# Spreading three reciprocal roots along the tokens by transfers through a line in DRAM instead of float32 products

## The chip, the cores and the metric

The kernel runs on one core of one Trainium2 chip. The metric is device time in microseconds (us) of one execution. The core has a matrix engine (TensorE: PE for the products, PEld for its weight loads), VectorE (DVE), ScalarE (ACT), GpSimd (POOL) and SyncE (SP). SP, ACT and POOL each issue DMA transfers in the order of their own instructions.

## The reference

One layer of a bidirectional encoder, for 512 tokens of width 2048. The input is normed, projected once, and split into queries, keys, values, a gate for attention, the input of a linear recurrence (LRU) and its gate. Attention and the recurrence (forwards and backwards) run side by side; each result is normed over its 1024 channels, gated and projected back.

```python
def rms_norm(x, w):
    xf = x.astype(jnp.float32)
    y = xf * lax.rsqrt(jnp.mean(xf * xf, axis=-1, keepdims=True) + EPS)
    return (y * w.astype(jnp.float32)).astype(x.dtype)

h = rms_norm(x, norm_w)
proj = jnp.einsum('bsd,de->bse', h, w_in)
q, k, v, g_attn, xr, g_lru = jnp.split(proj, SPLITS, axis=-1)
attn_out = attention_group(q, k, v, q_norm_w, k_norm_w)
lru_out = lru_group(xr, conv_w, conv_b, lru_wa, lru_ba, lru_wx, lru_bx, lru_lambda)
mixed = jnp.concatenate([rms_norm(attn_out, attn_norm_w) * jax.nn.silu(g_attn),
                         rms_norm(lru_out, lru_norm_w) * jax.nn.silu(g_lru)], axis=-1)
return x + jnp.einsum('bse,ed->bsd', mixed, w_out)
```

Three of these norms concern us: that of the input `x`, that of `lru_out` and that of `attn_out`. Each needs one reciprocal root per token.

## The kernel before

**Products.** Every float32 product is made of three products of float32r operands (`mm3`, lines 145 to 147): each operand is split into a rounded part (cast on ACT, line 204) and the rest (subtraction on DVE, line 205). Weights come in blocks of 256 rows by 512 columns (`wload`, a 512 KB transfer on SP's queue, line 193, three buffers `wr`). A projection (`proj_feat`, `proj_tok`) accumulates over eight such blocks in the four PSUM banks `pj`; the other four banks are `mm`.

**Order of the program.** The start loads `x` in eight chunks (line 223; the first in two halves), turns them on PE (`xturn`, line 230) and multiplies meanwhile (`a1`: LRU input, first half; the first products are line 287). 13 and 6 products on constants (`busy`, line 923) lie ahead of them, and the 16 rows of `norm_w` (`nw_st`, issued by ACT at line 937) are turned into the columns `nw`, which scale `x`. Then come the recurrences (`lru_half`, twice, woven into the next projections), keys and values (`kv`, woven into the query projections), attention (woven into the gate projections), and the output projection with fewer products than the plain one (`outputs`, line 890, with sums of weight blocks `ts` made by POOL's transfers in DRAM, lines 735 and 738).

**Norms.** A root is first a tile of 128 partitions by 4: token `t*128 + p` is at partition `p`, column `t`. The products need it along the free dimension and on all partitions. `rows` does this: four DVE instructions multiply the identity by a column each (line 265), one float32 product with ones spreads the diagonal over all partitions (line 267), and DVE copies it from PSUM (line 268). It runs three times: for `rbc` (root of the input, used by `evac_bc`, line 366), and twice for `gbc` (root of the LRU group, used by `normed`, line 655, on the tiles `hs`; later root of the attention group, on `av`). The roots themselves are made on POOL (lines 256 and 257). For the two groups, the sums over channels are products with a column of ones (`group_rstd`, line 643), four for every tile of squares; `lru_squares` leaves two such tiles, the halves of `hsum`.

**What sets the order.** PE's order is that of the text. SP's, ACT's and DVE's orders are that of the text in the first part of the start (scopes `s1`, `s2`) and in the output projection; elsewhere a scheduler orders by priority (`high_priority` moves a step ahead of its place) among what can be issued. Buffers of a tag are handed out in the order of the text. The tag `k2` of the pool `lru` has 12 buffers; its first tile is the diagonal of `xstats`, and the next are the gate weights `gr` of `lru_half` (lines 376 and 377, two 128 KB transfers for each of four blocks), which have a priority 600 steps ahead of their place. Each DMA from SP and ACT takes the next of eight semaphores (`DMAHW0` to `DMAHW7`) and waits until the transfer that had it before has landed.

Of the kernel before, what the change touches and what calls it, by code (L numbers as in the profile page):

```python
# [10 lines left out]
F32 = mybir.dt.float32  # L11
F32R = mybir.dt.float32r
AF = mybir.ActivationFunctionType
ALU = mybir.AluOpType
AX = mybir.AxisListType

P = 128
SEQ = 512
DM = 2048
KT = DM // P  # L20
NT = SEQ // P
# [34 lines left out]
def hybrid_kernel(  # L56
# [20 lines left out]
    nc = tc.nc  # L77
# [4 lines left out]
    pools, order = {}, {"left": [], "right": []}  # L82

    def opened(name, side):
        pools[name] = tc.alloc_tile_pool(name=name, bufs=1, side=side, reuse_waits="tile")
        order[side].append(name)
        return pools[name]
# [16 lines left out]
    dp = ctx.enter_context(tc.tile_pool(name="dp", bufs=1, space=bass.MemoryType.DRAM))  # L104
# [3 lines left out]
    def nm(s):  # L108
        cnt[0] += 1
        return f"{s}_{cnt[0]}"  # L110
# [4 lines left out]
    def work():  # L115
        return ("lru", LRU_K2, LRU_B4) if "lru" in pools else ("att", ATT_K2, ATT_B4)

    def k2(dt=F32, shape=(P, SEQ)):
        pool, n, _ = work()
        return pools[pool].tile(list(shape), dt, tag="k2", bufs=n, name=nm("k2"))  # L120
# [14 lines left out]
    def mm():  # L135
        return ps.tile([P, SEQ], F32, tag="mm", name=nm("mm"))

    def const(shape, name, dt=F32):
        return cp.tile(list(shape), dt, tag=name, name=name)

    def f(ap):
        return ap.bitcast(F32)
# [7 lines left out]
    ident = const([P, P], "ident")  # L150
    make_identity(nc, ident)
    ones = const([P, P], "ones")
# [101 lines left out]
    def rsqrt_mean(dst, src, n, width):  # L254

        nc.gpsimd.tensor_scalar(dst, src, 1.0 / n, EPS, op0=ALU.mult, op1=ALU.add)
        nc.gpsimd.tensor_tensor(dst, dst, nhalf[:, :width], op=ALU.pow)

    rstd = const([P, NT], "rstd")
    rbc = const([P, SEQ], "rbc")  # L260

    def rows(dst, col, dg):

        for t in range(NT):
            nc.vector.tensor_scalar(dg[:, t, :], ident, col[:, t : t + 1], None, op0=ALU.mult)
        pb = mm()
        nc.tensor.matmul(pb, ones, dg.rearrange("p t q -> p (t q)"), start=True, stop=True)
        nc.vector.tensor_copy(dst, pb)

    def xstats():  # L270
        s = const([P, NT], "xsum")
        nc.vector.reduce_sum(s, ssq, axis=AX.X)
        rsqrt_mean(rstd, s, DM, NT)
        rows(rbc, rstd, k2(shape=(P, NT, P)))

# [80 lines left out]
    sums = {}  # L358
# [93 lines left out]
    def lru_squares():  # L452

        hsum = pools["rot"].tile([P, 2, SEQ], F32, tag="hsum", name="hsum")
        nc.scalar.activation(hsum, hp[0], AF.Square)
        for pair in hp[1:]:
            yield 2
            sq = pools["rot"].tile([P, 2, SEQ], F32, tag="hsq", bufs=1, name=nm("hsq"))
            nc.scalar.activation(sq, pair, AF.Square)
            nc.vector.tensor_add(hsum, hsum, sq)  # L460
        sums["l"] = [hsum[:, k, :] for k in range(2)]


    def rope_consts():
# [25 lines left out]
    def norm_rope(es, nh, tab):  # L490

        es = [e[:, : nh * HD].rearrange("p (h d) -> p h d", d=HD) for e in es]
        rs = []
        for e in es:
            r = pools["rot"].tile([P, nh], F32, tag=f"rr{nh}", bufs=NT, name=nm("rr"))
            for h in range(nh):
                sq = pools["rot"].tile([P, HD], F32, tag="sh", bufs=1, name=nm("sh"))
                nc.scalar.activation(sq, e[:, h, :], AF.Square, accum_out=r[:, h : h + 1])
            rsqrt_mean(r, r, HD, nh)
            rs.append(r)  # L500
        for t, (e, r) in enumerate(zip(es, rs)):
            sq = pools["rot"].tile([P, nh, HD], F32, tag="sq", bufs=2, name=nm("sq"))
            nc.vector.tensor_mul(e, e, r[:, :, None].broadcast_to([P, nh, HD]))
            for s in range(2):
                nc.vector.tensor_mul(
                    sq.rearrange("p h (a s d) -> p h a s d", s=2, d=32)[:, :, :, s, :],
                    e.rearrange("p h (a s d) -> p h a s d", s=2, d=32)[:, :, :, 1 - s, :],
                    tab[:, t, 1, :].rearrange("p (a s d) -> p a s d", s=2, d=32)[:, None, :, s, :]
                    .broadcast_to([P, nh, 2, 32]),
                )  # L510
            nc.vector.tensor_mul(e, e, tab[:, t, 0, :][:, None, :].broadcast_to([P, nh, HD]))
            nc.vector.tensor_add(e, e, sq)
        return es
# [5 lines left out]
    def turn(rot, h):  # L519

        pt = mm()
        for t in range(NT):
            nc.tensor.transpose(pt[:, t * P : (t + 1) * P], rot[t][:, h, :], ident)  # L523
        return pt

    def split_ps(pt, hi, lo):
        nc.scalar.copy(hi, pt)
        nc.vector.tensor_sub(lo, pt, f(hi))

    def kv(es):  # L530
        rot = norm_rope(es, NKV, rk)
        yield 20
        opened("wx", "right")
        for t in range(NT):
            vv = es[t][:, NKV * HD :]
            vt = pools["qkv"].tile([P, 2, NKV * HD], F32R, tag="v", bufs=NT, name=nm("v"))
            vh[t], vl[t] = vt[:, 0, :], vt[:, 1, :]
            nc.scalar.copy(vh[t], vv)
            nc.vector.tensor_sub(vl[t], vv, f(vh[t]))
        yield from lru_squares()  # L540
        for h in range(NKV):
            yield (16, 4)[h]
            kt = pools["qkv"].tile([P, 2, SEQ], F32R, tag="kt", bufs=NKV, name=nm("kt"))
            kth[h], ktl[h] = kt[:, 0, :], kt[:, 1, :]
            split_ps(turn(rot, h), kth[h], ktl[h])
        r = group_rstd(sums["l"], "r_l", NB * P)
        yield 4
        rows(gbc, r, pools["rope"].tile([P, NT, P], F32, tag="kv", bufs=NT, name=nm("kv")))

    def turned(rot, h):  # L550

# [83 lines left out]
    def fin_s(shape=(P, SEQ)):  # L635
        return pools["fin"].tile(list(shape), F32, tag="s", bufs=2, name=nm("s"))

    def group_rstd(src, name, n):

        pr = mm()  # L640
        for t in range(NT):
            for k, part in enumerate(src):
                nc.tensor.matmul(
                    pr[:, t : t + 1], part[:, t * P : (t + 1) * P], ones[:, 0:1],
                    start=k == 0, stop=k == len(src) - 1,
                )
        r = const([P, NT], name)
        nc.vector.tensor_copy(r, pr[:, :NT])
        rsqrt_mean(r, r, n, NT)
        return r  # L650

    gbc = const([P, SEQ], "gbc")
# [294 lines left out]
    for step in proj_feat(C_XR, a1, first, given):  # L947
        if step is None:
            with tc.high_priority():
                first.append(wsplit(raw, 1))  # L950
                xturn(xc, 1)
            xsquare(xc, 0)
            next(next(loads), None)
            given[1] = wload(w_in, 2 * P, C_XR)
            continue
        c, e = step
        if (e == 0 or e == 2) and c:
            next(next(loads, iter(())), None)
        if (e, c) == (2, 0) or (e == 1 and c) or (e, c) in ((3, 1), (3, 2)):
            next(next(turns, iter(())), None)  # L960
        if (c, e) == (1, 2):
            given[2] = wload(w_in, 4 * P, C_XR)
            s2.close()
        if (c, e) == (2, 3):
            vec_load()
        if (c, e) == (5, 3):
            columns(vec, vec_st)
        if (c, e) == (KT // 2 - 1, 0):
            with tc.high_priority():
                xstats()  # L970
# [31 lines left out]

    fill = both()
    weave(fill, kv(kvs))
    drain(fill)

# [29 lines left out]
    r = group_rstd([sums["a"]], "r_a", NH * HD)  # L1036
    closed("att", "qkv")
    opened("fin", "right")
    for _ in range(3):
        next(fill)  # L1040
    rows(gbc, r, fin_s((P, NT, P)))


    def build(i, pair, where):
# [97 lines left out]
```

## Time and profile before

| | |
|---|---|
| median of 3 runs | 663.28 us (661.22 to 663.5) |
| the profiled execution | 663.34 us, of which the span in the profile is 661.5 us |
| PE, PEld | 654.1 us (99%), 540.6 us (82%) |
| DVE, ACT, POOL | 490.6 us (74%), 346.0 us (52%), 91.8 us (14%) |
| DMA | 96.19 MB, 145 GB/s over the span |
| chain that ended last | PE 88%, DVE 4%, issue 3%, DMA 3%, POOL 1% |

A row of the profile names the line, the engine, the operation and the tiles, then count, busy time, mean time of one, and what the engine waited for before it. Times in the timeline and in the chain count from the span's start. A PE row's time overlaps the next row's; the chain shows the pitch. An ending "q" (SPq) is the engine's queue, where transfers are issued; "us to landing" counts from the issue.

### The profile page before, as it was taken

What the parts mean: (1) busy time and instruction counts of PE and PEld (TensorE: products, weight loads), DVE (VectorE), ACT (ScalarE), POOL (GpSimd) and SP (SyncE); (2) the same over time, 40 slices, a digit from 0 to 9 for tenths busy, and PEclk for the clock granted to TensorE, in tenths of its full rate; (3) what the DMA queues carried; (4) which work ended last, traced back from release to release, by engine and by line L of the source; (5) the groups of instructions that cost most, each with busy time, mean ns of one, the idle gap of its engine ahead of it and who ended that gap; (6) DMA issues with size and microseconds to landing.
All of it is one profiled execution on the core that took longest, in us unless ns stands there. A gap on an engine that the chain in (4) does not pass through costs nothing.

```text
span 661.5 us, 8826 instructions
## 1 busy us (share of the span) xinstructions
PE 654.1 (99%) x3067; PEld 540.6 (82%) x3067; DVE 490.6 (74%) x851; ACT 346.0 (52%) x639; POOL 91.8 (14%) x121
## 2 busy tenths in 40 slices
PE   8999999999999999999999999999999999999997
PEld 6888888888888888888888888888888878888875
DVE  4879688977687952855865569528967998698994
ACT  3543799489856514454644437435444564333441
POOL 0000000000012301223253335410000000010000
PEclk9999999999999999999999999999999999999999
DMA  8843252322334221345776768762355766585322
GB/s 289 272 143 96 65 141 90 97 64 64 83 106 151 81 90 32 97 138 149 152 168 164 216 128 180 176 153 79 89 164 207 264 215 216 211 290 192 125 83 95
DMA packets 52732, 96.19 MB, mean 145 GB/s; under 512 B 4184, under 2 KB 14544, under 8 KB 52560
## 3 DMA queue, kind: packets, MB, share of 16 engines
q1 hardware_dynamic: 45648, 75.17, 36.0%
q0 software_dynamic: 6720, 19.93, 13.1%
q10 hardware_dynamic: 320, 0.53, 0.3%
q8 instruction: 24, 0.39, 0.2%
q14 instruction: 20, 0.16, 0.1%
HBM read 91.42 MB, written 20.97 MB: 170 GB/s over the span
## 4 chain that ended last, share of the span: by engine, by line
PE 88%; DVE 4%; issue 3%; DMA 3%; POOL 1%; ACT 0%; DVEq 0%; ACTq 0%; POOLq 0%
PE pj L145 19%; PE pj L147 19%; PE pj L146 19%; PE mm L890 9%; PE pj L890 7%; PE mm L146 3%; PE mm L147 3%; PE mm L145 3%; DVE ol L705 2%; PE mm L575 2%; DMA rw<-ts 2%; PE mm L230 1%; PE pj L287 1%; PE mm L523 1%; DMA nw_st<-in_norm_w_dram 1%
## 5 line engine op out<-in xcount | busy, mean ns | idle before, releaser
L145 PE MATMUL pj<-x,wh 128*128 128x512 f32 x376 | 150.2, 400 | 0.0
L147 PE MATMUL pj<-x,wl 128*128 128x512 f32 x376 | 147.1, 391 | 0.0
L146 PE MATMUL pj<-x,wh 128*128 128x512 f32 x376 | 146.7, 390 | 0.0
L204 ACT CAST wh<-wr 128x512 fp32r<-128x512 f32 x144 | 86.5, 617 | 75.9 <-PE pj L147 29.0
L205 DVE TENSOR_TENSOR wl<-wr,wh 128x512 fp32r<-128x512 f32 x144 | 99.5, 711 | 30.7 <-ACT wh L204 30.5
L147 PEld LDWEIGHTS pj<-x,wl 128*128 128x128 f32 x376 | 70.6, 188 | 15.4
L146 PEld LDWEIGHTS pj<-x,wh 128*128 128x128 f32 x376 | 70.8, 188 | 14.0 <-issue 0.5
L145 PEld LDWEIGHTS pj<-x,wh 128*128 128x128 f32 x376 | 70.7, 188 | 13.8 <-issue 0.5
L145 PE MATMUL pj<-wh,x 128*128 128x512 f32 x192 | 75.7, 394 | 0.0
L146 PE MATMUL pj<-wl,x 128*128 128x512 f32 x192 | 75.3, 392 | 0.0
L147 PE MATMUL pj<-wh,x 128*128 128x512 f32 x192 | 75.2, 392 | 0.0
L704 ACT CAST oh<-rw 128x512 fp32r<-128x512 f32 x94 | 54.8, 619 | 31.8 <-PE mm L890 14.5
L705 DVE TENSOR_TENSOR ol<-rw,oh 128x512 fp32r<-128x512 f32 x94 | 60.6, 686 | 9.2 <-ACT oh L704 6.8
L890 PE MATMUL mm<-ol,mh 128*128 128x512 f32 x128 | 50.2, 392 | 0.5 <-DVE ol L705 0.5
L890 PE MATMUL mm<-oh,mh 128*128 128x512 f32 x128 | 50.3, 393 | 0.0
L890 PE MATMUL mm<-oh,ml 128*128 128x512 f32 x128 | 50.2, 392 | 0.0
L577 ACT CAST b<-mm 128x512 fp32r<-128x512 f32 x32 | 18.7, 585 | 58.7 <-PE mm L575 58.7
L563 DVE TENSOR_REDUCE mx<-mm 128x1 f32<-128x512 f32 x32 | 22.0, 688 | 31.2 <-PE mm L147 30.9
L145 PEld LDWEIGHTS pj<-wh,x 128*128 128x128 f32 x192 | 36.1, 188 | 8.1 <-issue 0.2
L146 PEld LDWEIGHTS pj<-wl,x 128*128 128x128 f32 x192 | 36.1, 188 | 8.1 <-issue 0.2
L147 PEld LDWEIGHTS pj<-wh,x 128*128 128x128 f32 x192 | 36.1, 188 | 7.9
L890 PE MATMUL pj<-oh,mh 128*128 128x512 f32 x96 | 37.8, 394 | 0.0
(207 smaller groups left out, 1153.7 us busy)
## 6 DMA issues: line engine op xcount, KB each, us to landing
wr<-in_w_in_dram SPq DMA_DIRECT2D x71, 512.0 KB, 3.7
rw<-in_w_out_dram SPq DMA_DIRECT2D x63, 256.0 KB, 3.9
ts<-in_w_out_dram POOLq DMA_DIRECT2D x24, 512.0 KB, 6.9
rw<-ts SPq DMA_DIRECT2D x31, 256.0 KB, 5.0
ts<-ts POOLq DMA_DIRECT2D x8, 512.0 KB, 5.7
xt<-in_x_dram SPq DMA_DIRECT2D x8, 512.0 KB, 8.2
b<-in_x_dram SPq DMA_DIRECT2D x7, 512.0 KB, 7.7
out_dram<-xt POOLq DMA_DIRECT2D x12, 256.0 KB, 3.0
```

The lines of the kernel that those rows point to most:

```text
L145: nc.tensor.matmul(acc, lh, rh, start=start, stop=False)
L146: nc.tensor.matmul(acc, lh, rl, start=False, stop=False)
L147: nc.tensor.matmul(acc, ll, rh, start=False, stop=stop)
L204: nc.scalar.copy(hi, raw[:, k, :])
L205: nc.vector.tensor_sub(lo, raw[:, k, :], f(hi))
L230: nc.tensor.transpose(pt[:, t * P : (t + 1) * P], xc[:, t, ks], ident)
L563: nc.vector.tensor_reduce(mx, sc, axis=AX.X, op=ALU.max, negate=True)
L575: nc.tensor.transpose(pt[:, s * P : (s + 1) * P], p[:, s * P : (s + 1) * P], ident)
L577: nc.scalar.copy(pth[:, :, tt], p3)
L704: nc.scalar.copy(hi, src)
L705: nc.vector.tensor_sub(lo, src, f(hi))
L890: nc.tensor.matmul(bank[name, s], lh[:, a, ts_], rh, start=i == 0 and j == 0, stop=i == 7 and j == 2,)
```

## The change

`rows` no longer uses DVE, PE and PSUM. It writes the 128 x 4 tile into a line of 512 numbers in DRAM with one transfer from POOL's queue, in token order, and reads this line back into all 128 partitions with a second. `xstats` and the other callers give it no tile for the diagonal any more. In `lru_squares`, DVE adds the two halves of `hsum` first, so that `group_rstd` makes four products for the LRU group in place of eight.

```diff
-    def rows(dst, col, dg):
-
-        for t in range(NT):
-            nc.vector.tensor_scalar(dg[:, t, :], ident, col[:, t : t + 1], None, op0=ALU.mult)
-        pb = mm()
-        nc.tensor.matmul(pb, ones, dg.rearrange("p t q -> p (t q)"), start=True, stop=True)
-        nc.vector.tensor_copy(dst, pb)
+    def rows(dst, col):
+
+        line = dp.tile([1, SEQ], F32, tag=nm("line"), bufs=1, name=nm("line"))
+        nc.gpsimd.dma_start(line.rearrange("o (t p) -> p (o t)", p=P), col)
+        nc.gpsimd.dma_start(dst, line.broadcast_to([P, SEQ]))
...
-        rows(rbc, rstd, k2(shape=(P, NT, P)))
+        rows(rbc, rstd)
...
-        sums["l"] = [hsum[:, k, :] for k in range(2)]
+        nc.vector.tensor_add(hsum[:, 0, :], hsum[:, 0, :], hsum[:, 1, :])
+        sums["l"] = [hsum[:, 0, :]]
...
-        rows(gbc, r, pools["rope"].tile([P, NT, P], F32, tag="kv", bufs=NT, name=nm("kv")))
+        rows(gbc, r)
...
-    rows(gbc, r, fin_s((P, NT, P)))
+    rows(gbc, r)
```

The order of instructions changes with it, in more places than the text. Lines after `rows` have a number lower by 2 in the changed kernel (those after `lru_squares`, by 1). The first place is SP's queue at the very start: rows of `b` are chunks of `x`, `wr` weight blocks, `k` the gate weights. Before:

```order
L223 DMA b_18_139<-in_x_dram 128x4x128 x2
L223 DMA b_35_195<-in_x_dram 128x4x256
L193 DMA wr_197<-in_w_in_dram 128x2x512
L223 DMA b_47_255<-in_x_dram 128x4x256
L223 DMA b_54_291<-in_x_dram 128x4x256 [waits DMAHW0_49]
L193 DMA wr_293<-in_w_in_dram 128x2x512 [waits DMAHW1_49]
```

And now:

```order
L374 DMA k_122_672<-in_lru_wa_dram 128x2x128
L374 DMA k_123_675<-in_lru_wa_dram 128x2x128
L374 DMA k_124_678<-in_lru_wa_dram 128x2x128
L374 DMA k_125_681<-in_lru_wa_dram 128x2x128
L375 DMA k_122_672<-in_lru_wx_dram 128x2x128
L375 DMA k_123_675<-in_lru_wx_dram 128x2x128 [waits DMAHW0_49]
L375 DMA k_125_681<-in_lru_wx_dram 128x2x128 [waits DMAHW1_49]
L375 DMA k_124_678<-in_lru_wx_dram 128x2x128 [waits DMAHW2_49]
L223 DMA b_18_139<-in_x_dram 128x4x128 [waits DMAHW3_49]
L223 DMA b_18_139<-in_x_dram 128x4x128 [waits DMAHW4_49]
L223 DMA b_35_195<-in_x_dram 128x4x256 [waits DMAHW5_49]
```

The eight transfers of gate weights moved from rows 26 to 33 of this queue, behind all of `x`, to rows 1 to 8, ahead of it. No tile of `xstats` is now taken from the tag `k2` before them. `DMAHW0` is the semaphore of ACT's first weight block, `DMAHW3` that of `nw_st`.

The second place is DVE's start, where `nw` are the columns of `norm_w`, `wl` the rest of a split weight block, `x` the rest of a turned chunk. Before:

```order
L181 COPY nw<-mm_148 128x16
L205 TENSOR_TENSOR wl_152<-wr_141,wh_151 128x512
L233 SCALAR_TENSOR_TENSOR x_25_161<-mm_155,nw,x_24_160 128x512
L205 TENSOR_TENSOR wl_179<-wr_141,wh_178 128x512
L233 SCALAR_TENSOR_TENSOR x_34_188<-mm_182,nw,x_33_187 128x512
```

And now:

```order
L390 TENSOR_TENSOR k_131_693<-k_122_672,k_130_692 128x512
L181 COPY nw<-mm_148 128x16
L205 TENSOR_TENSOR wl_152<-wr_141,wh_151 128x512
L233 SCALAR_TENSOR_TENSOR x_25_161<-mm_155,nw,x_24_160 128x512
L205 TENSOR_TENSOR wl_179<-wr_141,wh_178 128x512
```

The split of the first block of gate weights now stands ahead of all else on DVE (its cast is ACT's second instruction on data, behind the cast of the first weight block).

The third place is POOL at the root of the input, where `rr` are the roots of the keys' heads. Before:

```order
L256 TENSOR_SCALAR rstd<-xsum 128x4
L257 TENSOR_TENSOR rstd<-rstd,nhalf 128x4
L256 TENSOR_SCALAR rr_1683<-rr_1683 128x2
L257 TENSOR_TENSOR rr_1683<-rr_1683,nhalf 128x2
L256 TENSOR_SCALAR rr_1690<-rr_1690 128x2
```

And now:

```order
L256 TENSOR_SCALAR rstd<-xsum 128x4
L257 TENSOR_TENSOR rstd<-rstd,nhalf 128x4
L265 DMA line_618<-rstd 128x4x1
L266 DMA rbc<-line_618 128x512
L256 TENSOR_SCALAR rr_1678<-rr_1678 128x2
L257 TENSOR_TENSOR rr_1678<-rr_1678,nhalf 128x2
```

The two transfers stand right behind the root, the second waiting on POOL for the first to land; it is the same at the other two roots. PE's order loses the three products of line 267 and four of line 643, and is otherwise as before. DVE and ACT swap some neighbouring rows after the attention, where `hs` and `av` are split.

## The prediction

> **What bounds the kernel now.** I read the page first, then the waits of PE, then the chain of waits in order of time, then the timelines where the change acts. The page gives PE nearly the whole span, and the chain that ended last runs through PE for 88% of it:
>
> ```profile
> PE 654.1 (99%) x3067; PEld 540.6 (82%) x3067; DVE 490.6 (74%) x851; ACT 346.0 (52%) x639; POOL 91.8 (14%) x121
> ...
> PE 88%; DVE 4%; issue 3%; DMA 3%; POOL 1%; ACT 0%; DVEq 0%; ACTq 0%; POOLq 0%
> ```
>
> A busy PE need not be at its peak, so the waits of PE matter more. This is the whole list:
>
> ```profile
> PE mm L179 <- DMA nw_st<-in_norm_w_dram: 1.5, 1, 1.5
> PE mm L923 <- POOL ones L153: 1.1, 1, 1.1
> PE mm L890 <- DVE ol L705: 0.5, 1, 0.5
> ```
>
> PE waits twice in the first 6 us and for 0.5 us much later. Between, a PE instruction taken out is time won, and anything that makes PE start later is time lost, with nothing behind it to absorb it. The chain in order of time shows both ends of this (start, length, what):
>
> ```profile
> 1.20 4.21 DMA nw_st<-in_norm_w_dram
> 5.80 1.05 PE mm L230 x4
> 6.84 1.28 PE mm L923 x6
> 8.12 1.71 PE pj L287 x4
> 9.83 0.54 PE mm L230 x4
> 10.37 3.23 PE pj L287 x14
> ...
> 55.45 0.86 PE mm L267 x2
> ...
> 233.89 1.68 PE mm L643 x16
> ...
> 241.24 0.86 PE mm L267 x2
> ...
> 451.88 0.86 PE mm L267 x2
> ```
>
> The true work of PE begins at 5.80 us, with the turning of the first half chunk of `x`, and runs without a gap from there.
>
> **What goes away on PE.** Each product of line 267 takes 0.86 us of the chain (recorded as two passes, x2). Three of them: 2.58 us. The eight products of line 643 for the LRU group (x16) take 1.68 us; half goes: 0.84 us. Together 3.42 us, all on the path.
>
> **The start.** Here the change moves something that its text does not mention: eight transfers of gate weights now stand on SP's queue ahead of the first half chunk of `x`, and these transfers are what PE's first step needs. What a transfer takes to issue is shown by SP's timeline: three chunks of `x` in 1.54 us, and the same eight transfers, in their old place, in 4.05 us (38.35 to 42.40):
>
> ```profile
> 0.72 1.54 SPq L223 DMA_DIRECT2D b<-in_x_dram  x3
> ...
> 38.35 2.00 SPq L376 DMA_DIRECT2D k<-in_lru_wa_dram  x4
> 40.39 2.01 SPq L377 DMA_DIRECT2D k<-in_lru_wx_dram  x4
> ```
>
> So `x` is issued at 0.72 + 4.05 = 4.77 us at the earliest. It is later, because of the eight semaphores: the sixth of these transfers waits for ACT's first weight block, which let its cast go at 4.61 us (the timeline's next row), and two more follow, then `x`, at 0.51 us each: 4.61 + 3 x 0.51 = 6.1 us. (`x` itself waits for the semaphore of `nw_st`, which landed at 1.20 + 4.21 = 5.41 us; that is earlier.)
>
> ```profile
> 4.61 0.62 ACT L204 CAST wh<-wr 128x512 fp32r<-128x512 f32 x1 [0.82 <-DMA wr<-in_w_in_dram]
> ```
>
> How long until it lands is read from the rows of issues (KB each, median us to landing):
>
> ```profile
> b<-in_x_dram SPq DMA_DIRECT2D x7, 512.0 KB, 7.7
> out_dram<-xt POOLq DMA_DIRECT2D x12, 256.0 KB, 3.0
> ...
> b<-in_x_dram SPq DMA_DIRECT2D x2, 256.0 KB, 4.6
> ```
>
> and, for the 128 KB loads of gate weights alone, from the answer on line 376:
>
> ```profile
> DMA to landing us min/median/max: 2.8/3.7/3.9
> ```
>
> The same half chunk took 4.6 us in a queue filling with `x` and weights. Now some of what is ahead has drained by 6.1 us, so I take 3.9, between the 3.7 us of a 128 KB load and the 4.6, nearer the first: landing at 10.0, PE at work at 10.2 instead of 5.80 us, 4.4 us later. Bounds: 4.77 + 2.8 (no wait for a semaphore, and the shortest of the small loads), PE at 7.8, 2.0 us later; 6.1 + 7.7 (as slow as a whole chunk in a full queue), PE at 14.0, 8.2 us later.
>
> DVE's first row, the split of gate weights, does not set this: its second transfer is fifth on SP, issued near 0.72 + 4 x 0.51 = 2.8 us, landed near 6.5 us by the 3.7, then a cast and a subtraction of 0.6 and 0.7 us, so `nw` follows near 7.8, ahead of `x`. The next loads (chunk 1, weight block 1) follow at 0.51 us each as before, so the whole start shifts as a block. Freeing the DMA engines at 38 to 42 us gains nothing: PE waits for no transfer there.
>
> There is a second, smaller cost. PE is slow when it starts: four products of line 287 took 1.71 us at 8.12 (0.43 each), fourteen took 3.23 us at 10.37 (0.23 each), and the first four turns 1.05 us against 0.54 later. From 5.80 to 9.83 it ran at half speed, for 4.0 us. The constants' products end at 1.12 + 2.95 = 4.07 us:
>
> ```profile
> 1.12 2.95 PE L923 MATMUL mm<-ones 128*128 128x256 bf16 x13 [1.12 <-POOL ones L153]
> ```
>
> Now PE stands nearly idle from there until 10.2, 6.1 us rather than 1.7. Bounds: the slow stretch is as long as before (0), or twice as long (half of 4.0 us more: 2.0 us). I take 0.4, near the first, since the pause before did not prevent a slow stretch either. The Trainium skill (TensorE: Matmul & The Clock Gate, Part 1) says that the clock is at half after an idle window of about 3.4 us, and at full again after a busy window of that length which runs freely; an estimate from it is 3.4 to 6.8 us of slow work after the pause, 0.3 us less to 1.4 us more than before, and at its middle the sum below would be 664.9. The rows of the slow stretch agree with it; the granted clock of the page doesn't show it.
>
> **The transfers.** Nothing in this trace writes 512 separate numbers of 4 bytes. POOL's cost of issuing is 0.54 us for 128 rows and 1.09 for 256 (first row: stores, second: adding weight blocks in DRAM), so near 2.2 us for 512 pieces:
>
> ```profile
> L825 POOL DMA_DIRECT2D out_dram<-xt x12: 539/540/664, 549.1 to 653.0; - x12
> ...
> L738 POOL DMA_DIRECT2D ts<-in_w_out_dram x16: 1059/1092/1127, 305.0 to 436.0; - x16
> DMA to landing us min/median/max: 6.3/7.2/8.9
> ```
>
> A hop takes 3.0 us (the stores' row of issues) to 8.9 us (the longest of these additions), two hops 6.0 to 17.8 us. I take 8: two small transfers, 3.0 each, and 2 us for the pieces. The cover at each root:
>
> ```profile
> 44.35 1.04 POOL L257 TENSOR_TENSOR rstd<-rstd,nhalf 128x4 f32<-128x4 f32 x1
> ...
> 57.07 1.36 DVE L366 TENSOR_TENSOR ev<-pj,rbc 128x512 f32<-128x512 f32 x2
> ...
> 236.14 1.01 POOL L257 TENSOR_TENSOR r_l<-r_l,nhalf 128x4 f32<-128x4 f32 x1
> ...
> 242.86 2.36 DVE L655 TENSOR_TENSOR hs<-hs,gbc 128x1024 f32<-128x1024 f32 x2
> ...
> 256.00 0.69 DVE L205 TENSOR_TENSOR wl<-wr,wh 128x512 fp32r<-128x512 f32 x1 [4.17 <-ACT wh L204]
> ...
> 448.61 1.03 POOL L257 TENSOR_TENSOR r_a<-r_a,nhalf 128x4 f32<-128x4 f32 x1
> ...
> 468.45 1.22 DVE L655 TENSOR_TENSOR av<-av,gbc 128x1024 f32<-128x1024 f32 x1
> ```
>
> At the first, the root is there at 45.4 us. `rbc` is needed by `evac_bc`, which empties the banks `pj` for the next projection. That begins 18 products after 56.3 (55.45 + 0.86), at 60.4 us; its first bank needs one `ev` (0.68 us), so `rbc` may come at 59.7, and without the product of line 267 at 58.9: 13.5 us of cover for 8 (18 x 0.23 = 4.1). At the second, the root is there at 237.2 and used at 242.9, 5.7 us. The rest of 2.3 us falls on DVE, with weight splits queued behind it; DVE then stands idle for 4.17 us before the split at 256.0, so it catches up, and PE, which works on blocks split earlier, doesn't notice. At the third there are 18.8 us (449.6 to 468.4). POOL has no other work waiting at any of them.
>
> **DVE.** The diagonals and the copies out of PSUM go; DVE is on the path at none of the roots, so I count nothing. The added sum of the halves is one DVE instruction on 128x512, 0.69 us like that at 256.0. It stands some thirty DVE rows ahead of the copy of `r_l`, which hide it; without them it would cost 0.69 us. The swapped rows of DVE and ACT after the attention I put at nothing, within the 0.5 us that PE waits for line 705.
>
> **The sum,** from the profiled execution, 663.34 us (0.06 above the median 663.28, so the same thing): 663.34 - 3.42 + 4.4 + 0.4 = **664.7 us**, 0.2% slower, which is no change that a measurement of this kernel can tell: the bound is about 0.5%, 3.3 us, so 660.0 to 666.6.
>
> **The rivals.**
>
> *The start costs far more* (slower). The half chunk lands as late as a whole chunk does in a full queue, 8.2 us after, and PE's slow stretch is twice as long, 2.0: 663.34 - 3.42 + 8.2 + 2.0 = 670.1; with the 0.4 of the forecast, 668.5. It decides from a shift of PE's first turn by 6.7 us in all. For it: the eight transfers and ACT's blocks share the same DMA engines, which are full in this stretch. Against it: whatever is ahead has had 4 us more to drain. Chance 0.16; I name 668.5.
>
> *The row comes too late at the first root* (slower). If two hops take 17.8 us, 4.3 us over the cover of 13.5, PE waits at the first product of the next projection: 664.7 + 4.3 = 669.0. For it: 512 pieces of 4 bytes, of which no row tells. Against it: the stores, each of a hundred times the bytes, land after 3.0 us. Chance 0.07. The Trainium skill (DMA: Bandwidth & Descriptors, Specifications) says that for pieces under 512 bytes a DMA engine reads, modifies and writes; no row here shows such a write, and by that rule alone I would put this rival at 0.10.
>
> *The start is hidden* (faster). If the loads of gate weights cost neither the issue nor the landing of `x`, as the text of the change would have it, only PE's gain is left: 663.34 - 3.42 = 659.9. Against it: PE's first step needs `x`, and `x` is the ninth transfer of its queue. Chance 0.05.
>
> *The forecast,* with a shift between its lower bound (2.0) and 6.7 us: 661.9 to 666.6. Chance 0.72.
>
> **The numbers.** Predicted 664.7. The range reaches from 661.9, the lower bound of the start, to 669.0, which takes in both slow rivals as they are priced; what lies outside (the hidden start, the worst end of the first rival, two mishaps at once) I put at 0.15. Faster by over 0.5%: 0.05, the hidden start. Slower: 0.16 + 0.07, and 0.03 for the upper edge of the forecast: 0.26. Within: 0.69.
>
> **What would show it.** PE's first turn of line 230 near 10.2 us, waiting for a transfer of `x`; the eight transfers on SP first, `x` issued near 6.1; products of line 287 still at 0.43 us for some 4 us after; no line 267 and half of line 643; the list of PE's waits otherwise unchanged; from line 257 to `ev` no wait of DVE for `rbc` that PE feels. The prediction is wrong if PE starts before 8 or after 13 us, if PE waits for `ev` near 65 us, or if PE's pitch changes after the attention.

## The result and the profile after

The changed kernel takes 666.73 us (median of 6 runs, 666.2 to 667.6) against 663.16 us for the kernel before (6 runs, 661.22 to 663.96): a ratio of 1.0059, 95% interval 1.0049 to 1.0070. That is inside the predicted range and 2.0 us above the predicted number. It is 0.1 us above the forecast's own upper end (666.6); the range reaches further because it takes in the two slow rivals. At 0.59% it lies just past the half per cent that tells a difference.

The profiled execution took 666.88 us, its span 664.9 us. Fourteen PE instructions are gone, and PE's share is lower all the same:

```profile
PE 651.8 (98%) x3053; PEld 538.7 (81%) x3053; DVE 485.6 (73%) x837; ACT 345.8 (52%) x639; POOL 96.5 (15%) x127
```

The list of PE's waits (total us, times, longest) says why. Of its five rows two are new, one for `x` at the start and one for `ev`, the output of `evac_bc` that `rbc` scales:

```profile
PE mm L230 <- DMA b<-in_x_dram: 4.4, 1, 4.4
PE pj L145 <- DVE ev L364: 2.3, 2, 1.4
...
PE mm L179 <- DMA nw_st<-in_norm_w_dram: 0.5, 1, 0.5
...
```

**The start.** The chain of waits in order of time (start, length, what) goes through the gate weights' last issues and then `x`:

```profile
0.72 3.33 DMA wr<-in_w_in_dram
...
4.07 0.37 SPq L375
...
5.50 3.75 DMA b<-in_x_dram
...
9.30 1.12 PE mm L230 x4
...
11.70 1.71 PE pj L285 x4
13.41 0.85 PE mm L230 x4
14.26 3.70 PE pj L285 x14
```

PE's first turn begins at 9.30 instead of 5.80 us, 3.50 later. From there to the end of the fourteen products (14.26 + 3.70 = 17.96) it takes 8.66 us; before it took 7.80 (5.80 to 10.37 + 3.23). So after the start PE is behind by 3.50 + 0.86 = 4.36 us.

**The first root.** The same view, 50 us in:

```profile
48.73 1.05 POOL rstd L257
49.78 0.31 issue
50.10 9.23 DMA line<-rstd
59.32 0.30 issue
59.62 4.71 DMA rbc<-line
...
64.43 0.70 DVE ev L364
...
69.88 0.61 DVE ev L364
...
70.54 0.50 PE pj L145
```

From the finished root (49.78) to the landed row (64.33) pass 14.55 us. PE, whose product of line 267 is gone, is 6.32 us behind after this place. So the place cost 2.80 us: 4.38 - 0.86 + 2.80 = 6.32, with 4.38 as PE's lag just ahead of it.

**The transfers** in the table of DMA issues (KB each, median us to landing):

```profile
gbc<-line POOLq DMA_DIRECT2D x2, 256.0 KB, 5.9
rbc<-line POOLq DMA_DIRECT2D x1, 256.0 KB, 4.7
...
line<-rstd POOLq DMA_DIRECT2D x1, 2.0 KB, 9.2
line<-r_l POOLq DMA_DIRECT2D x1, 2.0 KB, 9.6
line<-r_a POOLq DMA_DIRECT2D x1, 2.0 KB, 9.3
```

The 2 KB that go out take 1.6 to 2.0 times as long as the 256 KB that come back, at all three roots.

The trace also keeps the packets of each queue (q0 is POOL's, q1 is SP's). For the stretch from the issue of the first line at 50.1 us to 52.2 it has the first row below, beside a row of q1; for the stretch from there to the landing at 59.3 it has the second row and no other:

```profile
q0 software_dynamic: 32, 0.00, 8.1%
...
q1 hardware_dynamic: 64, 0.13, 12.7%
```

So POOL's 32 packets are over 2.1 us after the issue, and the other 7 us pass without one of that queue. Loads of others suffer as well: the two weight blocks that SP issues between 46 and 58 us took 8.9 us to land, where the two of the kernel before took 3.6 (first row before, second row now; min/median/max):

```profile
DMA to landing us min/median/max: 3.5/3.6/3.7
...
DMA to landing us min/median/max: 8.9/8.9/8.9
```

No row of PE's waits goes back to these blocks.

**The second root.** DVE waits 13.70 us for `gbc` (its timeline, idle time in brackets), and the products of line 642 are halved (the chain: 0.79 us against 1.68):

```profile
258.96 3.50 DVE L654 TENSOR_TENSOR hs<-hs,gbc 128x1024 f32<-128x1024 f32 x3 [13.70 <-DMA gbc<-line]
```

```profile
240.22 0.79 PE mm L642 x8
```

In the list of waits above, PE has no row for it, nor one at the third root.

**The account,** made on the spans: lag of the start +4.38, first root +2.80, three products of 0.86 and 0.89 of the halved sums -3.47, and -0.33 near 400 us, where a gap of the execution before does not come again (why is open): +3.38. The spans differ by 664.9 - 661.5 = 3.4.

### The profile page after: what moved, and what is told of

It reads as the page before. It is cut to its first block, busy times and chain, and to the rows that moved or that the text cites. A ratio compares the mean times of both kernels' runs of the same rounds, so it can differ in the third digit from the quotient of the medians.

```text
span 664.9 us, 8792 instructions
## 1 busy us (share of the span) xinstructions
PE 651.8 (98%) x3053; PEld 538.7 (81%) x3053; DVE 485.6 (73%) x837; ACT 345.8 (52%) x639; POOL 96.5 (15%) x127
## 3 DMA queue, kind: packets, MB, share of 16 engines
q0 software_dynamic: 7056, 20.72, 13.5%
## 4 chain that ended last, share of the span: by engine, by line
PE 87%; DVE 5%; DMA 4%; issue 2%; ACT 1%; POOL 0%; SPq 0%; DVEq 0%
PE pj L145 19%; PE pj L147 18%; PE pj L146 18%; PE mm L889 9%; PE pj L889 7%; PE mm L147 3%; PE mm L146 3%; PE mm L145 3%; DVE ol L704 2%; PE mm L574 2%; DMA line<-rstd 1%; PE mm L230 1%; PE pj L285 1%; DMA rbc<-line 1%; PE mm L522 1%
## 5 line engine op out<-in xcount | busy, mean ns | idle before, releaser
L889 PE MATMUL mm<-ol,mh 128*128 128x512 f32 x128 | 50.1, 392 | 0.5 <-DVE ol L704 0.5
```

The costliest lines, as they stand in the source:

```text
L889: nc.tensor.matmul(bank[name, s], lh[:, a, ts_], rh, start=i == 0 and j == 0, stop=i == 7 and j == 2,)
```

## The experiments

All ratios are to the kernel before on the same chip.

**1. Put `x` first again.** The changed kernel, with one tile of the tag `k2` taken and written in `xstats`, so that the gate weights stand behind `x` on SP as before:

```diff
         rsqrt_mean(rstd, s, DM, NT)
+        hold = k2(shape=(P, NT, P))
+        nc.vector.tensor_scalar(hold[:, 0, 0:NT], rstd, 1.0, None, op0=ALU.mult)
         rows(rbc, rstd)
```

> The changed kernel with one tile of the tag k2 taken again in xstats (one small DVE write of the root into it), so that the loads of gate weights stand behind x again; the transfers through DRAM stay. Theory A (the start costs the 4.38 us that PE's turns are later by, and the late row 2.80 us more, independent of each other): PE's first turn back near 5.8 us, PE still waiting 2 to 3 us for ev, 666.73 - 4.38 = 662.3 us. Theory B (the late row alone is the loss, the start's delay is made up elsewhere): no change, 666.5 us.

662.71 us (12 runs, 660.96 to 664.73), ratio 1.0004 [0.9992, 1.0015]: 4.0 us less than the changed kernel (3.7, when each is taken against the kernel before on its own chip). Its list of PE's waits has these two at the first root (`lc` is a tile of the recurrence on DVE, queued with `ev`):

```profile
PE pj L145 <- DVE ev L366: 1.1, 1, 1.1
PE pj L145 <- DVE lc L349: 1.1, 1, 1.1
```

The wait for `x` is gone, and PE still waits 2.2 us at the first root. The order of eight loads that the change does not mention is worth more than everything that it removes.

**2. Only the loads first.** The kernel before, with the diagonal of `xstats` taken from another pool; nothing else changes but the place of the gate weights on SP:

```diff
-        rows(rbc, rstd, k2(shape=(P, NT, P)))
+        rows(rbc, rstd, pools["rope"].tile([P, NT, P], F32, tag="kv", bufs=NT, name=nm("kv")))
```

> The kernel before with the diagonal of xstats in a tile of the pool rope in place of the tag k2, and nothing else: products on PE as before, but the loads of gate weights go first on SP. Theory A: only the start is late, by 3.5 us at the first turn and by 4.4 us after the slow stretch, 663.16 + 4.38 = 667.5 us. Theory B: 663.2 us.

666.74 us (5 runs, 666.16 to 667.19), ratio 1.0061 [1.0049, 1.0073]: 3.9 us over the kernel before on the same chip (662.86). So this alone is as large as the whole loss. The chain at its start:

```profile
5.59 3.62 DMA b<-in_x_dram
...
9.26 1.12 PE mm L230 x4
10.37 1.28 PE mm L923 x6
11.65 1.71 PE pj L287 x4
13.36 0.49 PE mm L230 x4
13.85 3.22 PE pj L287 x14
```

The first turn has the shift of the changed kernel (9.26), but the fourteen products end at 17.07, not 17.96: here the slow stretch is no longer than before. The extra 0.86 us of the changed kernel is not a fixed price of the pause (experiment 6 has its cause).

**3. The first root on PE as before,** the other two by transfers, the halves added first; its diagonal comes from `k2`, so `x` is first too. `rows_pe` is `rows` of the kernel before:

```diff
-        rows(rbc, rstd)
+        rows_pe(rbc, rstd, k2(shape=(P, NT, P)))
```

> The changed kernel with the first root spread by the products on PE as before (its tile is of the tag k2 again, so the start is as before, too); the two others by transfers, and the halves added first. Theory A: the two later rows are hidden and only PE's gain is left, two products of 0.86 us and 0.89 us of line 643: 663.16 - 2.61 = 660.5 us. Theory B (DVE's wait of 13.7 us for gbc of the LRU group reaches PE): 662 us or more.

658.82 us (5 runs, 658.65 to 660.45), ratio 0.9949 [0.9937, 0.9962], half a per cent below the kernel before. The list of PE's waits has a row neither for `x` nor for `ev`; DVE still waits 14.33 us for `gbc`, and PE has no row for that either.

It is 1.7 us better than expected. In the profiled execution PE is quick from its first turn:

```profile
5.68 0.60 PE mm L230 x4
...
7.05 1.19 PE pj L293 x4
8.24 0.44 PE mm L230 x4
8.68 3.21 PE pj L293 x14
```

The fourteen products end at 11.89, where before they end at 13.60. That executions of one kernel differ in this would explain why the times of the kernel before gather near 661.3 and between 662.2 and 664; but one execution of each kernel was profiled, so that part is argued, not shown.

**4. The line in the tile's own order.** Experiment 1 with 128 pieces of 16 bytes instead of 512 of 4:

```diff
-        nc.gpsimd.dma_start(line.rearrange("o (t p) -> p (o t)", p=P), col)
+        nc.gpsimd.dma_start(line.rearrange("o (p t) -> p (o t)", p=P), col)
```

> As the kernel with the held tile (e1_hold), but the line in DRAM lies in the tile's own order, so that a partition's four numbers are one piece of 16 bytes: 128 pieces in place of 512 of 4 bytes; tokens get each other's roots. Theory C (the first hop's 9.2 us goes with the number of pieces, over a fixed 3 us): a quarter of 6.2 us and 3 us, 4.6 us to landing, no wait of PE for ev, 662.3 - 2.8 = 659.5 us. Theory D (it is a fixed cost of such a write on POOL's queue): still near 9 us and 662.3 us.

659.66 us (4 runs, 659.54 to 660.16), ratio 0.9954 [0.9940, 0.9968]; 3.05 us less than experiment 1, with no wait of PE for `ev`:

```profile
line<-rstd POOLq DMA_DIRECT2D x1, 2.0 KB, 2.4
line<-r_l POOLq DMA_DIRECT2D x1, 2.0 KB, 1.8
line<-r_a POOLq DMA_DIRECT2D x1, 2.0 KB, 1.8
```

The same 2 KB, about a quarter of the time and less. The late row is what the first root cost: the two causes add up, 659.66 + 2.80 + 4.38 = 666.8 against 666.73 (on chips whose medians of the kernel before differ by 0.3 us).

**5. Another queue.** Experiment 1 with the first transfer issued by ACT (one run):

```diff
-        nc.gpsimd.dma_start(line.rearrange("o (t p) -> p (o t)", p=P), col)
+        nc.scalar.dma_start(line.rearrange("o (t p) -> p (o t)", p=P), col)
```

> As the kernel with the held tile (e1_hold), but ACT issues the first transfer of each root (512 pieces of 4 bytes, as in the changed kernel); the second stays with POOL. Theory E (the 9 us belong to the pieces as the DMA engines write them): still 8 to 10 us to landing. Theory F (they belong to POOL's way of making transfers): near the 3.7 us of the small loads on SP.

665.95 us. The transfer takes as long (8.76 and 10.2 us), so POOL's queue is not the cause. The chain shows a side effect:

```profile
43.60 8.76 DMA line<-rstd
52.38 0.37 SPq L377
```

From ACT, the transfer takes its turn among the semaphores that SP's loads use as well, and the last of the gate loads waits on SP until it has landed. PE waits 5.7 us there (for `lc`, line 349).

What follows this wait bears on the start, too. Two stretches of 5 us behind it show PE's busy time with the number of its products in brackets, and, third from the end, the granted clock:

```profile
63.40:68.40 5.00, 5.00 (x12) 3.94 (x13) 4.96 (x11) 1.83 (x4) 0.00 (x0) 0.50 0.36 106
69.00:74.00 5.00, 5.00 (x24) 4.12 (x23) 4.55 (x7) 2.72 (x5) 0.00 (x0) 1.00 0.29 95
```

At a clock of 0.50 PE makes half as many products, one in 0.43 us. In the trace the clock is at half from 61.92 us, within the wait, to 68.74, 5.4 us after work begins again.

**6. Keep PE busy until `x` is there.** The changed kernel with more products on constants ahead of the first turn:

```diff
-WARM, WARM2 = 13, 6
+WARM, WARM2 = 42, 6
```

> The changed kernel with 42 products on constants at the start in place of 13, which fill PE's pause before the first turn at 9.3 us (42 x 0.227 = 9.5 us when slow, less when fast); all else as changed. Theory G (the pause makes the slow stretch): the first four turns in 0.5 us rather than 1.12, the first four products of the first block in 0.9 rather than 1.71, and 666.73 - 2.5 = 664.2 us. Theory H (the slow stretch is not of the pause): no change, or up to 0.5 us slower where the constants still run when x lands.

664.51 us (7 runs, 663.39 to 667.62), ratio 1.0040 [1.0022, 1.0058]: 2.2 us under the changed kernel, or 1.7 when each is taken against the kernel before on its own chip. The chain:

```profile
9.15 0.67 PE mm L230 x4
...
10.58 1.19 PE pj L285 x4
...
12.21 3.21 PE pj L285 x14
```

The fourteen products end at 15.42 instead of 17.96. The page's row of the granted clock shows full speed at the start of every kernel, because the trace's clock records begin only with the first grant of the full clock. This first record stands at 9.90 us in the kernel before, at 13.34 in experiment 2, at 15.23 in the changed kernel, at 4.56 in experiment 3 and at 4.98 here, each time where the slow products (0.43 us, as at 0.50 in experiment 5) end, or, in the last two, before the first turn. So the slow stretch is PE at half clock, and the extra 0.86 us is its later end. The Trainium skill (TensorE: Matmul & The Clock Gate, Part 1) says that the clock is halved after an idle window of about 3.4 us, and that the windows run freely, whenever the work begins. The traces agree: the slow stretch goes when the pause is filled, it comes in the middle of experiment 5 after a wait of 5.7 us, and the two whole stretches of one clock recorded there (58.03 and 6.83 us) are 17 and 2 times 3.41 us. With windows that run freely, experiment 2 and the changed kernel can have the same pause and slow stretches of different length. The runs spread widely (663.39 to 667.62), and the profiled one (663.67) is among the fastest, so what the filling saves is good to perhaps 1 us.

**7. The same for experiment 3:**

```diff
-WARM, WARM2 = 13, 6
+WARM, WARM2 = 18, 6
```

> The fastest so far (e3_pe_first: first root by products, two by transfers, halves added first) with 18 products on constants at the start in place of 13, so that PE doesn't pause for 1.4 us before nw_st lands at 5.4 us. Theory G: the slow stretch ends earlier in most runs, 658.8 us with less spread than 658.65 to 660.45. Theory H: the same time and spread as e3_pe_first.

658.78 us (5 runs, 658.54 to 660.37), ratio 0.9948 [0.9935, 0.9961], against 658.82: no difference that these runs can tell.

**8. Number of pieces or their neighbourhood?** Experiment 1 with the 512 numbers 64 bytes apart in a longer line (one run):

```diff
+    lines = [dp.tile([1, 16 * SEQ], F32, tag=nm("line"), bufs=1, name=nm("line")) for _ in range(3)]
+    for ln in lines:
+        nc.gpsimd.dma_start(ln.rearrange("o (p e) -> p (o e)", p=P), ones[:, :64])
...
-        line = dp.tile([1, SEQ], F32, tag=nm("line"), bufs=1, name=nm("line"))
-        nc.gpsimd.dma_start(line.rearrange("o (t p) -> p (o t)", p=P), col)
-        nc.gpsimd.dma_start(dst, line.broadcast_to([P, SEQ]))
+        line = lines.pop(0)
+        nc.gpsimd.dma_start(
+            line.rearrange("o (t p s) -> p (o t) s", p=P, s=16)[:, :, 0], col
+        )
+        nc.gpsimd.dma_start(dst, line[:, :SEQ].broadcast_to([P, SEQ]))
```

> As the kernel with the held tile (e1_hold), but the 512 numbers of 4 bytes are written 64 bytes apart into a line 16 times as long (filled with ones at the start), and the second transfer reads its first 512 numbers, so that most tokens get a wrong root. Theory I (the first hop's time goes with the number of pieces): still 8 to 10 us. Theory J (it comes from neighbouring pieces of different partitions in one stretch of memory): 2 to 4 us.

659.24 us. Its rows of issues:

```profile
line<-rstd POOLq DMA_DIRECT2D x1, 2.0 KB, 2.6
line<-r_l POOLq DMA_DIRECT2D x1, 2.0 KB, 2.3
line<-r_a POOLq DMA_DIRECT2D x1, 2.0 KB, 2.3
```

As many pieces, of the same 4 bytes, from the same queue: 2.3 to 2.6 us rather than 9.2 to 9.6. The trace again has 32 packets of POOL's queue within 2.2 us of the first issue, and here the landing follows at 2.6. So it is neither the number nor the size of the pieces that makes the time, but, as it seems, that they lie side by side; this line had also been written once before, at the start, which experiment 10 shares.

**9. All three roots by transfers, without the cost.** Experiment 4, and DVE reads the row with a stride of four numbers, so that each token has its root (`by_tok(a)` is `a.rearrange("q (t p) -> q t p", t=NT)`):

```diff
-                nc.vector.tensor_mul(e, a, rbc)
+                nc.vector.tensor_mul(by_tok(e), by_tok(a), rbc.rearrange("q (p t) -> q t p", t=NT))
...
-        nc.vector.tensor_mul(pair, pair, gbc[:, None, :].broadcast_to([P, 2, SEQ]))
+        o = pair.rearrange("q k (t p) -> q k t p", t=NT)
+        g = gbc.rearrange("q (p t) -> q t p", t=NT)[:, None, :, :].broadcast_to([P, 2, NT, P])
+        nc.vector.tensor_mul(o, o, g)
```

> The kernel with the held tile and the line in the tile's own order (128 pieces of 16 bytes), and now DVE reads rbc and gbc with a stride of four numbers, so that every token gets its own root: the whole computation, with all three products of line 267 gone. Theory K (the strided read costs DVE nothing that PE feels): the time of e4_piece16, 659.66, within 0.5; a product of ev stays near 0.70 us, one of normed near 1.2 us, PE waits for neither. Theory L (the stride halves DVE's rate on these rows): an ev at 1.4 us, four of them in a row at the first root, so PE waits up to 2 us for banks at each projection of the input group: 661.5 to 664. In this kernel PE does 0.86 us less than in e3_pe_first, and the slow first products cost it 1.7 us in the executions in which they come: 657.9 with a quick start, 659.7 with a slow one.

659.33 us (6 runs, 658.54 to 660.38; three near 658.6, three near 660.2), ratio 0.9948 [0.9932, 0.9964]. DVE does pay for the stride (groups of instructions, mean ns after the busy us):

```profile
L369 DVE TENSOR_TENSOR ev<-pj,rbc 128x512 f32<-128x512 f32 x24 | 25.6, 1068 | 3.0 <-PE pj L147 2.8
...
L661 DVE TENSOR_TENSOR hs<-hs,gbc 128x1024 f32<-128x1024 f32 x4 | 7.8, 1999 | 3.8 <-DMA gbc<-line 3.8
```

In the changed kernel these take 686 and 1220 ns. PE feels almost none of it: no wait for `ev`, and 0.4 us more for line 896 at the end. So theory L has the rate and theory K the time. It has 0.86 us less on PE than experiment 3, and isn't measurably better.

**10. Sixteen bytes apart.** Experiment 8 with `4 * SEQ`, `ones[:, :16]` and `s=4` (one run):

> As e8_spaced, with the 512 numbers 16 bytes apart rather than 64, in a line four times as long; most tokens get a wrong root. If what costs the time is that several pieces of 4 bytes fall into one stretch of 64 bytes, four still do here: the first hop takes between the 2.3 us of e8_spaced and the 9.2 us of the changed kernel, near 4 us if it goes with the number in one stretch (a quarter of the extra 6.9 us, on top of 2.3). If only direct neighbours hurt, it takes 2.3 to 2.6 us as in e8_spaced. If 16 neighbours or 4 are the same, 9 us.

659.75 us:

```profile
line<-rstd POOLq DMA_DIRECT2D x1, 2.0 KB, 3.4
line<-r_l POOLq DMA_DIRECT2D x1, 2.0 KB, 2.3
line<-r_a POOLq DMA_DIRECT2D x1, 2.0 KB, 2.5
```

Two of three are as with 64 bytes, the first 0.8 us longer. Four pieces in a stretch of 64 bytes cost next to nothing; in these runs the 7 us came only with neighbours closer than 16 bytes. The Trainium skill (DMA: Bandwidth & Descriptors, Specifications) says that pieces under 512 bytes are read, modified and written. All pieces of experiments 4, 8 and 10 are under 512 bytes, and their transfers took 1.8 to 3.4 us, less than most loads of this kernel; so that rule by itself does not foretell the 9 us. That neighbours in one stretch have to be written one after the other would fit the 7 us between the last packet and the landing; no run shows the writes themselves. In experiments 8 and 10 the line was also written once at the start. Experiment 4 is quick without that, but with pieces of 16 bytes, so a part of the earlier write in the other two is not ruled out.

## Why the prediction was right, and where it was not

**The direction and the main cause** were right: the eight loads ahead of `x` on SP decide the sign (experiments 1 and 2). But one of the prediction's own signs of being wrong did come, PE's wait for `ev` near 65 us. The number holds because the range was widened for the rivals, not because the forecast's account of the first root was right.

**The gain on PE,** 3.42 us, measured 3.47 (three times 0.86, and 0.89).

**The start,** 4.4 us, was 3.50 at the first turn. The landing was well taken (3.75 against 3.9), the issue was not: `x` went out at 5.50, not 6.1, because the sixth gate load waited for ACT's weight block to land, at 4.05 us in the chain. The prediction took the start of the cast, 4.61, for it.

**The slow stretch,** 0.4 us, was 0.86 in the profile. Only its bounds (0 to 2.0) were well founded: experiment 2 has the same pause and no extra. The clock records give the lengths, from the first turn to the full clock: 4.10 us in the kernel before (5.80 to 9.90), 4.08 in experiment 2 (9.26 to 13.34), 5.93 in the changed kernel (9.30 to 15.23); half of the last difference, 1.83 us, is 0.9, near the 0.86. Together with the step before, 4.8 us foretold and 4.38 found: two errors that nearly cancel, by luck.

**The transfers** are the step that failed, in the size of a term. The term "I take 8" for two hops was 14.55 us at the first root (9.23 + 4.71, and 0.61 of gaps on POOL), within its bounds of 6.0 to 17.8 but 1 us over the cover of 13.5; the sum had nothing for the first root, where 2.80 us came. The choice rested on the row of the stores, 256 KB in 3.0 us. It was the nearest row in kind, but size was no guide: 2 KB of scattered numbers took three times that. What was guessed as POOL's cost, 2.2 us to issue 512 pieces, was 0.95 at most; the time passes between the last packet and the landing.

**The price of lateness** was undersized too. One us past the cover cost PE 2.80 us: 1.4 for the first bank, 0.9 for a later one, since the rest of `evac_bc` then stood among splits of gate weights in DVE's row (in the chain of the changed kernel its last `ev` starts at 69.88, 5.5 us after the first), and the remainder in slower products around it (the first one after the second wait takes 0.50 us, not 0.23). The prediction's price for this, a us of wait for each us past the cover, counts only the first bank.

**The rivals.** "The row comes too late at the first root" came true in mechanism and place, at 2.80 instead of 4.3 us; it had 0.07, too little for a price that no row of the trace bounded well. "The start costs far more" did not come: the first turn shifted by 3.5, not 6.7. "The start is hidden" fell with experiment 2. **The second and third roots** were hidden as said, with far more waiting on DVE than the 2.3 us foretold.

With its terms as measured, the prediction's sum is 663.34 - 3.47 + 4.38 + 2.80 = 667.05, and 666.7 with the 0.33 us near 400 us; the profiled execution has 666.88.

## What to carry to other kernels

When a tile is taken out of a pool, look at what stood behind it: here a scratch tile had been holding back eight loads by accident, and its removal cost more than the products saved. Scattered writes of single numbers side by side in DRAM were slow here, and loads issued around them landed late; write each partition's numbers as one piece and let the reader permute, or leave the spread on the matrix engine where the result is needed within some 14 us. A wait that comes late by 1 us can cost three, when work that is ready by then is queued between the instructions that would have met it.

## What the hardware showed that was not expected

- A transfer of 512 numbers of 4 bytes, each next to one from another partition, took 8.5 to 10.4 us from POOL's queue at every root, and 8.8 and 10.2 from ACT's. At the first root of the changed kernel its packets were over after 2.1 us, and weight blocks issued around that time took 8.9 us to land instead of 3.6. At 16 bytes apart it took 2.3 to 3.4, at 64 bytes 2.3 to 2.6, and as 16-byte pieces 1.8 to 2.4. Where between 4 and 16 bytes the change lies was not tried.
- DVE products of float32 slow down by 1.6 when one operand is read with a stride of 16 bytes (686 to 1068 ns, 1220 to 1999 ns); all operands are cut into 4 by 128 there, which was not tried apart.
- PE's first products come quick or slow, a difference of 1.7 us or a little more, in kernels whose starts are written alike (experiments 3 and 4), as the full clock is granted at 4.56 or 10.32 us. A wait of 5.7 us in the middle of a kernel brought the half clock back for 6.83 us (experiment 5). Filling the pause took it away in the profiled execution where the pause is long (experiment 6); where it is short, nothing was to be seen (experiment 7).
